# A hybrid state-space and latent-attention layer on one core: mask rows in q and k, the query latent normalised ahead of its projection, gated squares summed by TensorE, a new order table, and idle matmuls at the end

## The chip, the core and the metric

The kernel runs on one core of one Trainium2 chip. The time is device microseconds (us) of one execution. An execution is profiled apart from the timed runs; its span goes from the first to the last instruction of the core.

## What is computed

One layer for 576 tokens (512 of a new prompt, 64 of a running stream with 256 cached positions), width 1024, fp32:

```
proj = rmsnorm(x) @ w_in                    # z 512 | xBC 1024 | dt 8 | cq 256 | ckv 128 + rope 32
y    = ssd_scan(conv(xBC), dt)              # 8 state-space heads
y    = rmsnorm((y + d_skip*x) * silu(z))    # gate, then a norm over 512 channels
q    = rmsnorm(cq) @ w_uq                   # 8 heads, 64 + 32 rotated
s    = q . keys * scale, masked by blocks of 64 positions; softmax; o = pr @ values
x    = x + [y, o] @ w_out
x    = x + (silu(h @ w_gate) * (h @ w_up)) @ w_down      # h = rmsnorm(x), 2816 wide
out  = rmsnorm(x)
```

Outputs are the layer's result, the new latent keys, the rotated keys and the state-space and convolution states.

## The kernel before

Tokens lie along the free axis and channels on the 128 partitions, so a product with a weight tile is a matmul of 128 columns of weights with two halves of 288 tokens. Each such product is made of three matmuls, since weights and activations are each split in a rounded high part and a rest (`hilo`, L142 to L146, and `weights`, L112 and L113). The gate and up projections save one product in eight by sums of their operands (`xop`, L779 to L786, and `gu`, L795 to L806).

The stages follow each other in this order: the first products of the input projection and their norms, the remaining input projection with the convolution, the z part with the state-space chunks, the projection of q and k of the first head pairs and the values, the softmax of four head pairs beside the products with w_out (`ps_o`), the sums for gate and up, the gate and up products and the down products in parts, and a final norm in two column parts of 320 and 256 tokens.

Five engines work on this, each with its own queue, strictly in order. What stands where in each queue is fixed by the table `ISSUE`: a list of program numbers for each engine, which `issue_in_order` turns into a fixed sequence. DMAs are issued by SP, POOL and ACT.

What the change touches:

- `gate` (L552 to L559): the state-space output is multiplied with silu(z) on VectorE (L556), squared on ACT (L558), and the four channel tiles of the squares are added by a VectorE reduction into `ssy` (L559; the trace shows its buffer as R). `norm_y` (L728 to L732) then sums over the 128 partitions with a matmul by ones for each half (`ps_ny`, L731).
- `pair_proj` (L581 to L605): for each pair of heads, `qs` and `ks` hold 64 content and 32 rope rows. `evac_q` (L594) takes the projected q out of PSUM and multiplies with `Rq`, the norm factor of the query latent and the scale; `evac_k` (L598) copies k on ACT. The rope rows of q come by four POOL DMAs (L588), those of k by one SP DMA.
- `scores` (L634 to L651): one matmul for each query block and head (L641, contraction over 96 rows), then a VectorE memset (L642) that writes -1e30 into the 64x64 corner that the mask closes.
- `soft` (L620 to L632): maximum on VectorE (L627), exponential with sum on ACT (L628), reciprocal and scaling on VectorE (L629, L631). Score tiles live in the three PSUM banks with the tag "sc"; a fourth score matmul waits until the exponential has read the first.
- `cat_tile` (L735) scales the state-space output with its norm factor `Ry` and splits it in the two parts of `cat_y` (L142, L144), which `ps_o` reads.
- `q_rope` (L397 to L413): two products `ps_qr` for the rotated part, each taken out of PSUM with a multiplication by `Rq` (L403), then six VectorE operations.
- the end (L1040 to L1095): the squares of the second column part are summed over partitions into one packed bank (`ps_n`, L1040), a short chain on ACT and VectorE makes the factor `Rp`, two banks `ps_r` spread it again by matmuls with rows of the identity (L1091), R is copied (L1092), and VectorE and POOL scale the output, which DMAs carry out.

Of the kernel before, what the change touches and what calls it, by code (L numbers as in the profile page):

```python
# [19 lines left out]
P = 128  # L20
# [34 lines left out]
def hybrid_layer_kernel(ctx: ExitStack, tc: tile.TileContext, a, o):  # L55
# [207 lines left out]
    def in_tile(t, m=P):  # L263
# [6 lines left out]
    k1, k2, kr1, kr2, kt, rr0, rr1, qt0, qt1 = (  # L270
        rotp.tile([P, T], F32, name=z) for z in ("k1", "k2", "kr1", "kr2", "kt", "rr0", "rr1", "qt0", "qt1")
# [23 lines left out]
    dve.tensor_scalar(Rq, Rq, SCALE, None, ALU.mult)  # L295
    dve.scalar_tensor_tensor(ckf[:, :T], ckr, col(C_KN), Rk, ALU.mult, ALU.mult)
# [255 lines left out]
    def gate(c):  # L552
# [6 lines left out]
        dve.tensor_reduce(ssy[:, tk], q.rearrange("p t l -> p l t"), AX, ALU.add)  # L559
# [486 lines left out]
    with tc.manual_schedule(engines={pe.engine, dve.engine, pool.engine, act.engine}):  # L1046
# [39 lines left out]

        pr1 = [lbank("sc", f"ps_r3_{z}", 1) for z in range(2)]
# [32 lines left out]
0-7 20-21 14-15 8-13 22-25 38-39 26-29 16-19 32-37 30-31 44-47 40-43 56-61 74 48-49 62-66 75-77 50-55 68 78 69 67  # L1120
80-83 79 70-73 86-89 92-97 84-85 98 110-115 128 134-135 90-91 104-109 122-127 142-146 129-133 148-153 147 99-103
116-121 136-141 154-171 174-182 270-274 172-173 183-269 275-370 373-415 371 416-420 372 421-612 637-640 613-617
641-642 657-660 618-636 665-702 643-644 703-712 661-663 713-722 763 723-742 664 764-766 645-652 743-760 653-656
761-762 771-794 767-770 795-828 837-844 851 829-831 833-834 872-873 832 835-836 854-856 845 874-875 846-848 852-853
849-850 857-859 880-883 888-891 884-887 860-862 913-914 863-871 876-879 892-900 915-916 923-925 917-922 926 901-903
927-928 904-912 946 929-933 947-948 934-943 949-950 944 951 945 952-957 985 969 958-965 997-1001 966-968 1002-1003
973-975 986-996 1004-1008 1011-1016 970-971 976-978 1025-1027 972 979-983 1017-1019 1041-1046 984 1028-1036 1020
1009-1010 1021-1024 1037-1038 1057-1061 1063-1067 1062 1068-1074 1039-1040 1047 1050-1052 1075-1079 1048-1049
1053-1055 1103-1105 1056 1087-1092 1080-1082 1093 1083-1086 1097-1101 1106-1114 1094-1096 1141-1143 1102 1139
1144-1150 1152-1157 1151 1140 1158 1115-1126 1159-1160 1127-1138 1161-1162 1166-1169 1163-1165 1172-1173 1211-1231  # L1130
1174 1232-1234 1175-1177 1170-1171 1187-1188 1178-1180 1235-1237 1247-1252 1238-1244 1181 1209 1184 1253-1255
1182-1183 1185-1186 1210 1245-1246 1256-1258 1189 1197-1202 1190-1196 1203-1205 1259-1260 1271-1282 1261 1206 1262
1207-1208 1283-1288 1263-1270 1289-1310 1324-1337 1311-1323 1338-1510 1518-1525 1557 1511 1526-1529 1554 1560
1512-1517 1558-1559 1530-1553 1561-1562 1578-1581 1555 1563-1565 1569-1571 1590-1592 1611-1613 1582-1583 1602-1604
1556 1575-1577 1596-1598 1617-1619 1584 1623-1624 1585-1586 1572-1574 1593-1595 1566-1568 1587-1589 1608-1610
# [150 lines left out]
```

## Time and profile before

| | |
|---|---|
| runs timed | 666.59, 667.73, 669.0 us; median 667.73 |
| the profiled execution | 667.77 us, its span 666.0 us, mean granted TensorE clock 0.986 |
| busy share of the span | TensorE 97%, VectorE 79%, ACT 49%, POOL 5% |
| chain that ended last, by engine | TensorE 84%, VectorE 10%, ACT 2%, issue 2%, DMA 1%, POOL 1% |

The granted clock is given as a share of 2.4 GHz: 1.00 is 2.4 GHz and 0.50 is 1.2 GHz. In rows of the trace, "[0.64 <-ACT pr L628]" is idle time just before a group of instructions and the instruction that ended it. A group's name is output<-inputs with its shapes, and "x4" is the count of instructions. An fp32 matmul shows as two instructions.

### The profile page before, as it was taken

The page shows a single profiled execution, that of the slowest core. Times are in us where ns is not written, and L with a number is a line of the kernel's source. Part 1 is how long each engine was busy: PE and PEld are TensorE (multiplying, and loading weights), DVE is VectorE, ACT ScalarE, POOL GpSimd, SP SyncE. Part 2 cuts the span into 40 slices and gives each one's busy share as a digit, 9 for nine tenths or more (in the row PEclk, how much of TensorE's full clock was granted, in tenths as well). Part 3 has the DMA queues.
Part 4 walks back from the last instruction along what each step waited for, and adds up shares of the span by engine and source line. Part 5 has one row for each costly group of instructions (what it writes and reads, how often), then busy time and mean ns, then how long its engine had stood idle before and what let it go on. Part 6 is the DMA issues. An engine that isn't in the chain of part 4 may idle for free.

```text
span 666.0 us, 11869 instructions
## 1 busy us (share of the span) xinstructions
PE 646.1 (97%) x4691; PEld 610.5 (92%) x4691; DVE 526.0 (79%) x994; ACT 329.0 (49%) x600; POOL 31.9 (5%) x72
## 2 busy tenths in 40 slices
PE   9999999997999998999999999999999999999994
PEld 9799999864778898999999999999999999999994
DVE  6998997999878599999978585775868586966563
ACT  8644437755564367647423454324533354335463
POOL 0010230101010000000000000000000000000004
PEclk9999999996999999999999999999999999999997
DMA  9323284331042333132411233321232224222004
GB/s 324 109 69 99 63 215 131 111 99 34 32 125 64 78 98 110 64 127 73 150 64 64 72 115 100 127 64 64 80 112 95 95 64 127 65 95 95 1 0 143
DMA packets 26184, 63.61 MB, mean 96 GB/s; under 512 B 3330, under 2 KB 10000, under 8 KB 25872
## 3 DMA queue, kind: packets, MB, share of 16 engines
q1 hardware_dynamic: 24144, 60.54, 29.4%
q0 software_dynamic: 752, 1.09, 0.7%
q10 hardware_dynamic: 1232, 1.23, 0.6%
q8 instruction: 37, 0.61, 0.4%
q14 instruction: 19, 0.16, 0.1%
HBM read 58.03 MB, written 3.30 MB: 92 GB/s over the span
## 4 chain that ended last, share of the span: by engine, by line
PE 84%; DVE 10%; ACT 2%; issue 2%; DMA 1%; POOL 1%; POOLq 0%; DVEq 0%; ACTq 0%
PE ps_x L838 19%; PE ps_d L939 17%; PE ps_z L838 9%; PE ps_in L128 8%; PE ps_y L838 5%; PE ps_z L432 4%; PE ps_o L432 3%; PE ps_first L128 3%; PE sc L641 2%; PE ps_l L939 2%; PE pv L689 2%; PE ptp L664 1%; DVE xop L786 1%; DVE fz L154 1%; DMA gu<-in_w_gu 1%
## 5 line engine op out<-in xcount | busy, mean ns | idle before, releaser
L939 PE MATMUL ps_d<-pr,wh_d 128*128 128x288 f32 x576 | 115.6, 294 | 0.0
L838 PE MATMUL ps_x<-xop,wh_gu_S 128*128 128x288 f32 x504 | 101.9, 295 | 0.3 <-ACT g L900 0.3
L939 PEld LDWEIGHTS ps_d<-pr,wh_d 128*128 128x128 f32 x576 | 92.5, 188 | 0.0
L939 PE MATMUL ps_d<-pr,wl_d 128*128 128x288 f32 x288 | 84.7, 295 | 0.0
L838 PEld LDWEIGHTS ps_x<-xop,wh_gu_S 128*128 128x128 f32 x504 | 80.6, 188 | 0.5 <-ACT g L900 0.5
L113 DVE TENSOR_TENSOR wl_gu_S<-gu,wh_gu_S 128x1024 fp32r<-128x1024 f32 x44 | 53.8, 1222 | 33.7 <-PE ps_y L838 13.8
L838 PE MATMUL ps_x<-xop,wl_gu_S 128*128 128x288 f32 x252 | 73.4, 295 | 0.0
L112 ACT CAST wh_gu_S<-gu 128x1024 fp32r<-128x1024 f32 x44 | 46.1, 1051 | 44.7 <-PE ps_d L939 25.4
L939 PEld LDWEIGHTS ps_d<-pr,wl_d 128*128 128x128 f32 x288 | 54.1, 188 | 0.0
L838 PEld LDWEIGHTS ps_x<-xop,wl_gu_S 128*128 128x128 f32 x252 | 47.0, 188 | 0.0
L112 ACT CAST wh_d<-wr_d 128x640 fp32r<-128x640 f32 (+1 forms) x32 | 21.6, 675 | 48.4 <-PE ps_x L838 23.6
L128 PE MATMUL ps_in<-xs,wh_in 128*128 128x288 f32 x256 | 45.4, 298 | 0.0
L838 PE MATMUL ps_z<-xop,gu_a 128*128 128x288 f32 x252 | 38.7, 296 | 0.0
L128 PEld LDWEIGHTS ps_in<-xs,wh_in 128*128 128x128 f32 x256 | 37.8, 189 | 0.3
L838 PE MATMUL ps_z<-xop,wh_gu_S 128*128 128x288 f32 x168 | 36.3, 296 | 0.0
L838 PE MATMUL ps_x<-xop,wh_gu_A 128*128 128x288 f32 x168 | 35.5, 297 | 0.0
L838 PEld LDWEIGHTS ps_z<-xop,gu_a 128*128 128x128 f32 x252 | 35.3, 188 | 0.1
L838 PE MATMUL ps_y<-xop,wh_gu_A 128*128 128x288 f32 x168 | 35.1, 296 | 0.0
L952 DVE TENSOR_TENSOR x<-ps_d,x 128x288 f32<-128x288 f32 x64 | 28.6, 452 | 6.6 <-PE ps_d L939 6.2
L800 ACT CAST gu_a<-gu 128x512 fp32r<-128x512 f32 x22 | 13.7, 621 | 37.6 <-PE ps_x L838 18.0
L112 ACT CAST wh_gu_A<-gu 128x1024 fp32r<-128x1024 f32 x22 | 23.1, 1048 | 18.3 <-PE ps_d L939 11.5
L113 DVE TENSOR_TENSOR wl_gu_A<-gu,wh_gu_A 128x1024 fp32r<-128x1024 f32 x22 | 26.9, 1221 | 5.2 <-PE ps_x L838 3.9
(328 smaller groups left out, 1625.7 us busy)
## 6 DMA issues: line engine op xcount, KB each, us to landing
gu<-in_w_gu SPq DMA_DIRECT2D x44, 512.0 KB, 3.9
wr_d<-in_w_down SPq DMA_DIRECT2D x16, 320.0 KB, 3.0
wr_in<-in_w_in SPq DMA_DIRECT2D x8, 512.0 KB, 4.6
wr_out<-in_w_out SPq DMA_DIRECT2D x8, 512.0 KB, 3.3
wr_d<-in_w_down SPq DMA_DIRECT2D x16, 256.0 KB, 2.7
cumb<-cumD SPq DMA_DIRECT2D x5, 512.0 KB, 5.2
x<-in_xT SPq DMA_DIRECT2D x2, 1152.0 KB, 7.0
wr_z<-in_w_in SPq DMA_DIRECT2D x4, 512.0 KB, 4.5
```

What stands on the lines that cost most here:

```text
L112: act.copy(hi, raw)
L113: dve.tensor_tensor(lo, raw, hi.bitcast(F32), ALU.subtract)
L128: pe.matmul(ps[:m, hf, :n], w, x[:, hf * n : (hf + 1) * n], start=start and k == 0 and i == 0, stop=stop and k == last and i == 2,)
L154: dve.tensor_tensor(ssq, ssq, q, ALU.add)
L432: pe.matmul(ps[:, :n], w, x[:, cols], start=k == 0 and i == 0, stop=k == len(terms) - 1 and i == 2,)
L641: pe.matmul(s[:, :nk], qs[:, j, q0 : q0 + P], ks[:, j, :nk], start=True, stop=True)
L664: pe.transpose(pp[:, k : k + P], prs[p, i][:, j, b * P : b * P + P], ident)
L689: pe.matmul(pv[64 * j : 64 * j + 64, b * P :], V[b][:, h * HD : (h + 1) * HD], pts[p, b, j], start=b == 0, stop=True, skip_group_check=b > 0,)
L800: act.copy(l(a22), r(r2))
L838: pe.matmul(ps, p, q, start=not onto and first and kp == kps[0] and j == 0, stop=onto or (last and kp == kps[-1] and j == 2), skip_group_c ...
L939: pe.matmul(ps, w, x[:, cols], start=first and k == 0 and i == 0, stop=last and k == len(terms) - 1 and i == 2,)
L952: dve.tensor_tensor(x2[t][:, cols], ps, x2[t][:, cols], ALU.add)
```

## The change

The core of the diff, line numbers of the new kernel being higher by 11 to 15 from the attention on:

```diff
+    qk_bufs = [
+        (qkp.tile([100, 2, T], F32, name=f"qs{i}"), qkp.tile([100, 2, NKEY], F32, name=f"ks{i}")) for i in range(2)
+    ]
+    for z, n, v, k0 in ((0, T, -1e30, 0), (1, NKEY, 1.0, 64)):
+        m = qk_bufs[0][z][96:100]
+        pool.memset(m, v)
+        for sign in (1, -1):
+            pool.affine_select(
+                out=m, in_=m, pattern=[[0, 2], [sign, n]], compare_op=ALU.is_ge, fill=0.0,
+                base=-k0 if sign > 0 else k0 + 63, channel_multiplier=-128 * sign,
+            )
+        pool.dma_start(qk_bufs[1][z][96:100], m)
...
     dve.tensor_scalar(Rq, Rq, SCALE, None, ALU.mult)
+    dve.tensor_tensor(cq, cq, Rq.unsqueeze(1).to_broadcast([P, 2, T]), ALU.mult)
...
-            dve.tensor_tensor(halves(rr[i]), ps[:, :, :TH], Rqh, ALU.mult)
+            rr.append(ps[:, :, :TH])
...
+        for i, (f, g, u, op) in enumerate(((c0, c1, qt0, ALU.subtract), (c1, c0, qt1, ALU.add))):
+            dve.tensor_tensor(halves(s[:, i]), rr[0], f, ALU.mult)
+            dve.tensor_tensor(halves(u), rr[1], g, ALU.mult)
+            dve.tensor_tensor(s[:, i], s[:, i], u, op)
...
         act.activation(q, yv, AF.Square)
-        dve.tensor_reduce(ssy[:, tk], q.rearrange("p t l -> p l t"), AX, ALU.add)
+        ps = bank("pp", f"ps_g{c}")[:, :L]
+        for t in range(4):
+            pe.matmul(ps, ones, q[:, t], start=t == 0, stop=t == 3)
+        act.copy(ssy[:, tk], ps)
...
-        qs = qkp.tile([96, 2, T], F32, tag="qs", name=f"qs{p}")
-        ks = qkp.tile([96, 2, NKEY], F32, tag="ks", name=f"ks{p}")
+        qs, ks = qk_bufs[p % 2]
...
-        sp.dma_start(ks[64:96], krall.unsqueeze(1).to_broadcast([ROPE, 2, NKEY]))
+        if p < 2:
+            sp.dma_start(ks[64:96], krall.unsqueeze(1).to_broadcast([ROPE, 2, NKEY]))
...
-                r = slice(64 * j, 64 * j + 64)
-                dve.tensor_tensor(qs[0:64, j, cols], ps[r], Rq[r, cols], ALU.mult)
+                (dve.tensor_copy if j else act.copy)(qs[0:64, j, cols], ps[64 * j : 64 * j + 64])
...
-                dve.memset(s[0:64, nk - 64 : nk], -1e30)
...
     def norm_y():
-        ps = [bank("hm", f"ps_ny{hf}") for hf in range(2)]
         for hf in range(2):
-            pe.matmul(ps[hf][:, :TH], ones, ssy[:, hf * TH : (hf + 1) * TH], start=True, stop=True)
-            norm_half(Ry[:, hf * TH : (hf + 1) * TH], ps[hf][:, :TH], 512)
+            cols = slice(hf * TH, (hf + 1) * TH)
+            norm_half(Ry[:, cols], ssy[:, cols], 512)
...
+        warm = bank("hm", "ps_warm_last")
+        for _ in range(7):
+            pe.matmul(warm[:, :P], ones, ones, start=True, stop=True)
...
 ISSUE = {
     "PE": """
-0-7 20-21 14-15 8-13 22-25 38-39 26-29 16-19 32-37 30-31 44-47 40-43 56-61 74 48-49 62-66 75-77 50-55 68 78 69 67
+0-7 14-15 8-9 20-23 16-17 10-13 26-27 24-25 38-42 18-19 32-37 43 56 28-31 44-45 57-61 74-79 92 46-49 62-67 80-84 50-55
...
```

Each mask row r of `qs` holds -1e30 on the first 64 queries of block r and 0 elsewhere, each of `ks` holds 1 on the last 64 keys of block r, so that the score matmul over 100 rows adds -1e30 where the memset wrote it. The two pairs of buffers are used in turn by the four head pairs, so the mask rows and the rope rows of the keys stay.

The new table moves work on every engine. At the start of the softmax TensorE's queue stood like this before, with the last products of q of the second head pair (`ps_q`) between scores of the first (`sc`), and the first norm sum (`ps_ny`); the score `sc_3_0` stands four rows further ahead:

```order
L641 MATMUL sc_3_1_1916<-ks_1745,qs_1744 128x512
L641 MATMUL sc_1_0_1941<-ks_1745,qs_1744 128x256
L432 MATMUL ps_q_0_1867<-cqn_470,wl_pair_1804 128x288
L432 MATMUL ps_q_0_1867<-cqn_473,wh_pair_1803 128x288 x2
L432 MATMUL ps_q_0_1867<-cqn_473,wl_pair_1804 128x288
L432 MATMUL ps_q_1_1882<-cqn_470,wh_pair_1803 128x288 x2
L432 MATMUL ps_q_1_1882<-cqn_470,wl_pair_1804 128x288
L432 MATMUL ps_q_1_1882<-cqn_473,wh_pair_1803 128x288 x2
L432 MATMUL ps_q_1_1882<-cqn_473,wl_pair_1804 128x288
L641 MATMUL sc_1_1_1944<-ks_1745,qs_1744 128x256
L641 MATMUL sc_2_0_1957<-ks_1745,qs_1744 128x384
L731 MATMUL ps_ny_1891<-R_99,ones 128x288
```

So three scores of the first pair stood ahead of the end of its neighbour's q. In the new kernel the queue is, from the end of the same product on, with the gated sums of the last two chunks as `ps_g`:

```order
L443 MATMUL ps_q_1_1912<-cqn_484,wl_pair_1826 128x288
L654 MATMUL sc_3_0_1939<-ks_383,qs_382 128x512
L654 MATMUL sc_3_1_1941<-ks_383,qs_382 128x512
L572 MATMUL ps_g_1876<-ysq_1874,ones 128x128
L654 MATMUL sc_1_0_1965<-ks_383,qs_382 128x256
L654 MATMUL sc_1_1_1967<-ks_383,qs_382 128x256
L572 MATMUL ps_g_1885<-ysq_1883,ones 128x128 x4
L654 MATMUL sc_2_0_1979<-ks_383,qs_382 128x384
L654 MATMUL sc_2_1_1981<-ks_383,qs_382 128x384
L654 MATMUL sc_0_0_1993<-ks_383,qs_382 128x128
L572 MATMUL ps_g_1876<-ysq_1874,ones 128x128 x3
```

All scores of the first pair now stand behind the last product of q, the gated sums stand between them, and the two norm sums are gone.

VectorE's queue at the same place before (evacuations of q, memsets, maxima `mx`, gated sums into R_99):

```order
L594 TENSOR_TENSOR qs_1807<-ps_q_0_1867,Rq 64x288
L642 MEMSET sc_3_1_1916 64x64
L594 TENSOR_TENSOR qs_1807<-ps_q_0_1867,Rq 64x288
L642 MEMSET sc_1_0_1941 64x64
L627 TENSOR_REDUCE mx<-sc_3_1_1916 128x1
L559 TENSOR_REDUCE R_99<-ysq_1858 128x128
L594 TENSOR_TENSOR qs_1807<-ps_q_1_1882,Rq 64x288
L642 MEMSET sc_1_1_1944 64x64
L627 TENSOR_REDUCE mx<-sc_1_0_1941 128x1
```

and in the new kernel:

```order
L607 COPY qs_384<-ps_q_0_1897 64x288
L567 TENSOR_TENSOR xsd<-xsd,sz 128x4x128
L640 TENSOR_REDUCE mx<-sc_3_0_1939 128x1
L567 TENSOR_TENSOR xsd<-xsd,sz 128x4x128
L640 TENSOR_REDUCE mx<-sc_3_1_1941 128x1
L640 TENSOR_REDUCE mx<-sc_1_0_1965 128x1
L607 COPY qs_384<-ps_q_1_1912 64x288
L640 TENSOR_REDUCE mx<-sc_1_1_1967 128x1
```

The reductions and memsets are gone, of each two evacuations one is left, and the last gated multiplication (L567) stands behind the first maximum.

At the end of the program TensorE's queue is now this, where before the two `ps_r` followed the packed sums directly:

```order
L1051 MATMUL ps_n_1_7355<-fz,ones 64x128 x2
L1051 MATMUL ps_n_1_7355<-sq,ones 64x128 x4
L1100 MATMUL ps_warm_last<-ones 128x128 x7
L1106 MATMUL ps_r_0_7545<-Rp,ident 128x128 x2
L1106 MATMUL ps_r_1_7546<-Rp,ident 128x128 x2
```

The seven idle matmuls multiply ones with ones, and nothing reads their result.

## Rows read from the trace of the kernel before

**Rows 1.** The page, busy time by engine
```profile
PE 646.1 (97%) x4691; PEld 610.5 (92%) x4691; DVE 526.0 (79%) x994; ACT 329.0 (49%) x600; POOL 31.9 (5%) x72
```
**Rows 2.** Stretches: length, busy PE, PEld, DVE, ACT, POOL, clock, DMA share, GB/s
```profile
140.00:148.00 8.00, 7.76 (x37) 5.46 (x35) 7.80 (x16) 4.14 (x9) 0.00 (x0) 1.00 0.52 154
148.00:154.00 6.00, 3.44 (x11) 1.59 (x11) 5.77 (x16) 4.56 (x13) 0.00 (x0) 1.00 0.17 69
154.00:166.00 12.00, 9.77 (x27) 4.94 (x26) 11.57 (x35) 5.68 (x17) 2.25 (x4) 0.57 0.18 48
166.00:226.00 60.00, 60.00 (x422) 48.47 (x422) 47.41 (x141) 32.81 (x90) 1.92 (x4) 1.00 0.20 62
...
234.00:271.00 37.00, 34.22 (x248) 32.77 (x247) 36.86 (x67) 26.27 (x41) 0.00 (x0) 1.00 0.26 88
```
**Rows 3.** Waits of TensorE: total us, times, longest
```profile
PE sc L641 <- ACT pr L628: 3.0, 5, 1.1
...
PE ps_p L838 <- DVE xop L786: 1.8, 3, 1.1
```
**Rows 4.** Timeline of TensorE, 143 to 180 us: start, us, group
```profile
143.24 1.12 PE L641 MATMUL sc<-ks,qs 96*128 96x512 f32 x2
...
147.80 0.29 PE L432 MATMUL ps_q<-cqn,wl_pair 128*128 128x288 f32 x1
...
165.72 0.51 PE L432 MATMUL ps_o<-cat_y,wh_out 128*128 128x288 f32 x2
...
171.52 0.49 PE L664 MATMUL ptp<-ident,pr 128*128 128x128 f32 x3
...
172.96 0.71 PE L664 MATMUL ptp<-ident,pr 128*128 128x128 f32 x5
```
**Rows 5.** Timeline of VectorE, 133 to 169 us
```profile
145.92 0.69 DVE L627 TENSOR_REDUCE mx<-sc 128x1 f32<-128x512 f32 x1
...
166.61 0.76 DVE L144 TENSOR_TENSOR cat_y<-xsd,cat_y 128x576 fp32r<-128x576 f32 x1 [1.00 <-ACT cat_y L142]
...
167.47 0.73 DVE L144 TENSOR_TENSOR cat_y<-xsd,cat_y 128x576 fp32r<-128x576 f32 x1
```
**Rows 6.** Single lines: count, ns min/median/max, first and last start
```profile
L559 DVE TENSOR_REDUCE R<-ysq x5: 593/1031/1074, 133.5 to 152.5; 128x128 f32<-128x512 f32 x4, 128x64 f32<-128x256 f32 x1
...
L594 DVE TENSOR_TENSOR qs<-ps_q,Rq x16: 431/454/461, 136.8 to 193.6; 64x288 f32<-64x288 f32 x16
...
L642 DVE MEMSET sc<- x32: 112/112/112, 144.5 to 214.4; 64x64 f32 x32
...
L731 PE MATMUL ps_ny<-R,ones x4: 403/406/481, 151.2 to 154.0; 128*128 128x288 f32 x4
```
**Rows 7.** Groups by form: busy us, mean ns, idle before
```profile
L403 DVE TENSOR_TENSOR rr<-ps_qr,Rq 128x576 f32<-128x576 f32 x2 | 1.5, 754 | 0.6 <-PE ps_qr L128 0.6
...
L489 POOL TENSOR_SCALAR_AFFINE_SELECT cumb<-cumb 128x1024 f32<-128x1024 f32 x4 | 4.4, 1093 | 22.2 <-ACT el L464 22.2
...
L322 POOL MEMSET dt<- 128x40 f32 x1 | 0.1, 132 | 23.4 <-DVE wl_in L113 23.4
```
**Rows 8.** Timeline of VectorE, 218 to 283 us
```profile
233.95 0.69 DVE L795 TENSOR_TENSOR gu<-gu 128x512 f32<-128x512 f32 x1 [1.56 <-DMA gu<-in_w_gu]
...
271.16 2.09 DVE L786 TENSOR_TENSOR xop<-xv,xop 128x576 fp32r<-128x576 f32 x3
```
**Rows 9.** Timeline of all engines, 651 us to the end
```profile
657.40 2.08 PE L1091 MATMUL ps_r<-Rp,ident 128*128 128x128 f32 x8 [1.90 <-DVE Rp L178]
...
659.51 0.37 ACT L1092 COPY R<-ps_r 128x256 f32<-128x256 f32 x1 [2.89 <-PE ps_r L1091]
```
**Rows 10.** Stretch of the end, columns as in rows 2
```profile
658.00:659.50 1.50, 1.48 (x7) 1.18 (x6) 0.84 (x3) 0.00 (x0) 0.00 (x0) 0.50 0.55 194
```
**Rows 11.** Timeline of TensorE, the first 5 us
```profile
1.00 3.78 PE L203 MATMUL ps_warm<-ones 128*128 128x128 f32 x16 [1.00 <-POOL nepsb L97]
```
**Rows 12.** Timeline of ACT, 143 to 170 us
```profile
148.58 0.62 ACT L558 ACTIVATE ysq<-xsd 128x512 f32<-128x512 f32 x1
```

More of the change, by code (lines that the diff above doesn't have):

```diff
@@ L246, in hybrid_layer_kernel @@
     ssq2, ssk = tmp("ssq2"), tmp("ssk")
+    Rq = tmp("Rq")
     for k in range(2):
@@ L267, in in_tile @@
         return ps[:m, :, :TH]
-    k1, k2, kr1, kr2, kt, rr0, rr1, qt0, qt1 = (
-        rotp.tile([P, T], F32, name=z) for z in ("k1", "k2", "kr1", "kr2", "kt", "rr0", "rr1", "qt0", "qt1")
+    k1, k2, kr1, kr2, kt, qt0, qt1 = (
+        rotp.tile([P, T], F32, name=z) for z in ("k1", "k2", "kr1", "kr2", "kt", "qt0", "qt1")
     )
@@ L398, in q_rope @@
         w = weights(a["w_uqr"], 512, "uqr")
-        rr = (rr0, rr1)
+        rr = []
         for i in range(2):
@@ L1125 @@
[L1125 to L1134, printed above, removed]
@@ new lines @@
+146-147 154-171 174-175 270-274 176-221 172-173 222-269 275-370 373-420 371 421-468 372 469-636 665-688 637-638
+641-644 639-640 657-658 689-735 737-742 736 743-760 659-660 645-656 661-664 771-818 763 767-770 764-766 761-762
+819-826 859-861 833-835 837 862-864 838 836 827-832 865-866 868-870 867 880-883 841 845-852 871-873 853-856 839-840
+842-844 874-876 884 877-879 885-886 904-909 857 887 858 888 892-899 910-912 900-903 889-891 913-915 925-926 916-924
+927-935 939-940 949-951 936-938 952-965 941 966-967 945-948 968-970 942-944 971-979 987 980-983 1003 988 1015-1016 984
@@ new lines @@
+991-993 985-986 989 1004-1009 1017-1021 1010-1011 1022-1024 1012-1014 1025-1026 994-999 1029-1034 1043-1045 1000-1002
+990 1046-1054 1035-1042 1059-1064 1027-1028 1075-1079 1055 1081-1092 1080 1065 1056 1066 1057 1067 1058 1093-1104 1068
+1121-1129 1069-1073 1130-1132 1105-1107 1133-1144 1074 1145-1156 1108 1229-1240 1111-1113 1119 1109-1110 1241-1246
+1253-1254 1114 1247-1248 1120 1157 1255-1260 1249-1252 1158 1115-1118 1159-1160 1261-1263 1161 1264 1176 1162-1175
+1177 1180 1265 1178 1184-1186 1181-1183 1187 1190-1192 1266-1274 1179 1188 1275-1276 1193-1198 1189 1199-1207
@@ new lines @@
+1215-1220 1208-1214 1221-1222 1227-1228 1277-1288 1223 1289-1296 1224-1226 1301-1303 1297-1300 1304-1322 1342-1343
+1348-1355 1344-1347 1323-1341 1356-1479 1572 1575 1480-1496 1573 1497-1523 1578 1524-1535 1574 1576 1536-1538
+1579-1580 1539-1547 1584 1581-1582 1587 1585 1599 1583 1548-1552 1577 1560 1602-1604 1553-1559 1561-1563 1588-1589
+1564-1571 1593-1595 1614-1616 1635-1637 1608-1610 1629 1586 1605-1607 1626-1628 1647 1590-1592 1611 1630-1631 1650
+1612-1613 1632 1648-1649 1600-1601 1620-1622 1641-1643 1596-1598 1617-1619 1638-1640 1651 1623-1625 1644-1645 1656
@@ new lines @@
+222 225 216-217 211 220 218 212-213 226 219 221 301 233 227-228 223 234 229-232 237 235 245 236 246 256 238 257 247
+316 248-249 261 258 262 260 239 266 259 240 267 263 241 265 264 242 271 243 268 244 269-270 274 250 252 275 272 251
+273 254 253 279 255 280-281 296 283 276 297 282 302 284 293 288 294 289 285 287 277-278 304 327 290-291 298 315 286
+305 328 306 292 310 326 311 329 312 307 303 337 314 317 313 318 338 378 321 299-300 309 308 339 332 379 322 330 333
+323 319 334 380 331 340-341 320 325 336 348 335 342 344-345 343 346-347 324 383 349 353 350 358 352 354 364 351 365
@@ new lines @@
+355 381 360 356 366 393 371 382 359 367 357 373 361 374 370 368-369 384 362 375-376 363 377 372 386-387 385 388-389
+392 391 390 398 406 394 399 395 400 402 401 403 413 396 404 421 397 405 409 407 411 410 412 419 408 415 417 414 416
+418 436 420 424 422 425 423 426 429 427-428 432-434 431 478 485 437 435 439 430 440 438 441 480 442-443 481 444 454
+479 447-448 450 449 452 451 453 445 455 458 456 446 457 459 482-483 460 467 462 484 461 468 463 489 469 471 470 464
+493 491 486 465 564 472 490 492 494 473 496 504 488 474 495 497 505-506 508 487 569 501 576 507 466 589 475 503 509
@@ new lines @@
+198-199 203 212 222 215 214 213 218 228 206 229-230 254 231-232 219-220 226 221 255 225 224 227 235 234 233 236-240
+242 245-246 241 247 261 250 243-244 248-249 252-253 251 256-258 260 259 267 263-265 268 270 266 276 269 274 262
+271-272 285 273 275 277-278 283 280-281 279 282 312 284 286 313 287 292 288-289 293 295 291 294 290 296 299 297-298
+300-301 314 302-303 315 319 304-305 320 306-308 316 309 318 317 321-323 328-329 326 330 327 310 331-332 324 337 311
+338 335 339 336 341 340 333 346-347 344-345 348 325 334 349 357-358 342 350 354 351 343 359 353 352
@@ L1185 @@
+65 67 66 76 71 70 78 69 73 64 86-87 75 74 88 80 84-85 89-91 98 101 99-100 102-103
 """,
```

82 lines of the change are left out of this document (25 added, 57 removed).

## The prediction

> **What bounds the kernel now.** I read the busy shares, then the stretches, then the waits of TensorE, and last the timelines where it waits. TensorE is busy 97% of the span [rows 1], so a gain can only come from the few places where it waits or runs at the lower clock. The stretches show them [rows 2]. Up to 148 us and from 166 to 226 us it is full, and the clock is at 1.00. From 148 to 154 us it is busy 3.44 of 6 us, and from 154 to 166 us the granted clock is 0.57 on average, that is mostly 1.2 in place of 2.4 GHz. VectorE is busy 5.77 of 6 and 11.57 of 12 us there: this is the start of the softmax, where VectorE has maxima, scaling, gated sums, evacuations and the norm of the state-space output at once. TensorE's largest wait is there too: 3.0 us in which score matmuls wait until the exponential frees a bank [rows 3], and the exponential waits for VectorE's maximum. From 234 to 271 us VectorE is busy 36.86 of 37 us, and the gate and up products wait 1.8 us for their summed operands [rows 2, 3]. At the end the two `ps_r` run 2.08 us in eight instructions, at a clock of 0.50, after an idle time of 1.90 us [rows 9, 10]. Behind 271 us and ahead of 148 us nothing is to be had from order alone.
>
> **The softmax start, before.** The last product of q ends at 148.1 us, the first maximum starts at 145.92, the fourth split of `cat_y` ends at 168.20, and the products with w_out run densely from 165.72 [rows 4, 5]. So VectorE takes 22.28 us from the first maximum to the fourth split, with 1.00 us idle.
>
> **What the change adds on TensorE.** An fp32 matmul of 128 columns is two instructions; five such take 0.71 and three 0.49 us, so each adds 0.11 us [rows 4]. A gated sum of a full chunk is four matmuls, 8 x 0.11 = 0.88 us, the half chunk half of it: 4.5 chunks are 3.96 us. The `ps_ny` go: two matmuls, four instructions of 0.25 us each in steps, 1.0 us (a single one is listed with 406 ns, of which the overlap is taken off) [rows 6]. Net 2.9 us. 2.5 chunks (2.2 us) lie ahead of the end of q, where TensorE is full, but three score tiles (512, 512 and 256 columns, 2 x 10 pieces of 128 columns x 0.11 = 2.2 us) move behind it. So q ends again at about 148.0, and the added 2.9 us fall in the stretch in which TensorE has room: 6 - 3.44 us up to 154 alone.
>
> **What it takes from VectorE.** Four gated reductions of 1.03 and one of 0.59 us (4.7 us), half of the 16 evacuations of 0.45 (3.6 us), and 32 memsets of 0.11 us, which mostly overlap and which I count at 0.06 (1.9 us) [rows 6]. ACT gets eight copies; it is busy 49% [rows 1], and only 4.56 of 6 us in the tightest stretch [rows 2]. Of these savings the ones in full stretches count. After the first maximum: two gated sums 1.9, three of four evacuations 1.2, ten memsets 0.6, the idle 1.0 (the splits now have ACT's part further ahead), together 4.7. Against it one more 128x512 maximum in front of the splits, 0.6, and a gated multiplication less, 0.6. So 22.3 - 4.7 = 17.6 us; summing the new queue's instructions by the same durations gives 17.0. I take 17.3. The first maximum cannot start until `sc_3_0` is done: 148.0 + 0.9 + 0.1 = 149.0 us. The fourth split then ends at 166.3, not 168.2: **-1.9 us**. Behind it, TensorE's remaining work up to the next common point is 0.66 us less, since pair 1's scores have been moved ahead: I take 0.5. **Sum for this stage: -2.4 us.** The ends: nothing, if the chain is as long as before; and -6.8 if TensorE alone decides: its work from the end of q to `ps_o` is 34 pieces of 128 score columns x 0.22, the sample scores 0.5, two gated sums 1.76 and eight transposes 1.76, 11.5 us, so `ps_o` at 159.6 in place of 165.72, and the 0.66. The value lies nearer to VectorE's sum, since VectorE is the one that is full in these rows.
>
> **166 to 226 us.** TensorE is full, VectorE 47.41 of 60 us [rows 2]. 22 memsets and eight evacuations leave VectorE; hidden, so 0. The shift passes through.
>
> **234 to 271 us.** The stage begins when the first gate and up weights land, at 233.95, and the last summed operands are done at 273.25 [rows 8]: 39.3 us of VectorE. Priced with the steps at which the same kinds follow each other there, the new queue has 0.8 us less ahead of the last operand: a weight split of the following group now stands behind it, and running sums of squares stand elsewhere. **-0.8 us**; bounds 0 and -1.8, the whole wait [rows 3].
>
> **The end.** The seven idle matmuls follow the packed sums at 655.50 and take 14 x 0.11 = 1.5 us, up to 657.0, ahead of the 657.40 at which `Rp` is there [rows 9]. TensorE is then idle 0.4 in place of 1.90 us. If the clock stays at 1.00, `ps_r` takes 8 x 0.13 = 1.04 and not 2.08 us; R's copy, the last scaling and the DMAs behind it move with it: **-1.0 us**. The Trainium skill has a rule that speaks against this (TensorE: Matmul & The Clock Gate, section "The HAM clock gate"): the clock falls after a whole window without work, so one short gap would not lower it, and the idle matmuls would be worth nothing. The row shows 0.50 behind a gap of 1.90 us, so the measurement decides; by the page the term would be 0.
>
> **Costs I set to nothing.** The mask rows: POOL gets two memsets, four selections and two DMAs at the start. A selection over 1024 elements takes 1.09 us, so 4 x 1.1 to 1.8, with the memsets under 9 us, inside the 23.4 us in which POOL waits for the time-step rows [rows 7]; key DMAs queued behind them are needed far later. If that cover were gone, the first scores would wait for `ks`. Four more contraction rows: 0. The query norm: one multiplication over 1152 columns, twice 0.75 less the overlap, 1.4 us, against the two of 0.754 that go [rows 7]; the normalised latent must now wait for its norm factor, and its last part stands some fifteen VectorE instructions ahead of the one that reads the first product made of it. `ps_qr` stays longer in PSUM; VectorE is next to read it. Two SP DMAs go. New orders ahead of 148 us: 0, TensorE has no room there to gain.
>
> **Sum:** -2.4 - 0.8 - 1.0 = -4.2 us on the profiled execution's 667.77 us, which is as good as the median (667.73): **663.5 us**. About 2 us, 0.3%, is what a measurement of this kernel can tell from no change.
>
> **Rivals.**
>
> *The clock falls again (0.20).* In 148 to 154 us TensorE was busy 57% of the time and the clock fell after it [rows 2]. The new order has 11.5 us of work up to `ps_o`, about 70% of the time, but still in short groups that wait for banks. If half of it runs at 1.2 GHz, that adds 5.7 us: 148.0 + 11.5 + 5.7 = 165.2, only 0.5 to 1 us better than now; with 0.8 and 1.0 that is 665.3. The Trainium skill names such a case on the same page (section "A second HAM failure mode: psum-queue depth-cycling"): groups that cycle through PSUM banks leave TensorE idle for short times, and the clock goes up and down. Rows 2 agree with it for the kernel before.
>
> *The chain of the softmax is not shorter (0.13), and the kernel slower.* TensorE's queue now holds `ps_g_1885` between score tiles. It waits for ACT's square of a gated product that stands on VectorE behind the first maximum: 149.0 + 0.6 + 0.6, then the square of 0.62 [rows 12], and about as much for an exponential ahead of it: 151.5. The scores `sc_2_0` and later stand behind it. If the round from bank to maximum to exponential sets the pace and not VectorE's sum, the chain keeps its 22.3 us but starts at 149.0, not 145.92 [rows 5]: +3.1, with -1.0 at the end and nothing at 234 us, 669.9. It decides if VectorE shows idle times of over 4 us in sum between the first maximum and the fourth split.
>
> *TensorE decides (0.12).* -6.8, -1.8 and -1.0: 658.2. For it: VectorE loses 4.7 us exactly where it is full. Against: the scaled probabilities still come late in VectorE's queue.
>
> *The idle matmuls run slowly (0.07).* At the start of the kernel 16 such instructions took 3.78 us, 0.236 each [rows 11]. 14 of them would end at 658.8, 1.4 us after `Rp`: 667.77 - 3.2 + 1.4 = 666.0.
>
> **How the numbers follow.** My forecast has 0.48. Its own range is 661.5 to 665.7: the chain's 17.0 to 17.6, the middle term 0 to -1.8, the end 0 to -1.0. Faster by over 0.3% (under 665.7) takes in nearly all of it, the third rival and half of the first: 0.69. Slower by over 0.3% (over 669.8) is half of the second rival and a little for waits that a new order of five queues may open anywhere: 0.13. The rest, 0.18, is no change. The range 659 to 669 leaves out half of the second and half of the third rival and the unnamed.
>
> **What would show it.** In the changed profile: first maximum at about 149, fourth split at about 166, `ps_o` dense from about 163, granted clock 1.00 through 154 to 166 us; `ps_r` in about 1.0 us at a clock of 1.00; the last summed operand some 3 us earlier than 273.25. A clock near 0.5 at the softmax, or VectorE idle there, would put the first term wrong; `ps_r` still at 2 us the last; a TensorE wait over 1 us ahead of 148 us the assumption that the new order costs nothing.

## The result and the profile after

The changed kernel takes **656.54 us** (median of 4 runs, 655.98 to 659.61) where the kernel before took 667.65 beside it: ratio **0.984 [0.981, 0.988]**, 11.1 us faster. The forecast was 663.5 us in a range of 659 to 669: the sign was right, the time lies below the range, and the gain is 2.6 times the one forecast. The profiled execution after took 656.87 us, its span 655.2, which is 10.8 us less than the span before; the steps below are made from the two spans.

The page, busy time by engine, of the kernel after:

```profile
PE 641.5 (98%) x4741; PEld 612.5 (93%) x4741; DVE 516.0 (79%) x948; ACT 332.7 (51%) x613; POOL 43.8 (7%) x80
```

Against [rows 1] TensorE has 4.6 us less and VectorE 10 us less, but the shares hardly move. Stretches of the kernel after, columns as in [rows 2]:

```profile
148.00:154.00 6.00, 6.00 (x28) 3.58 (x27) 5.88 (x14) 5.27 (x15) 0.00 (x0) 1.00 0.94 310
154.00:166.00 12.00, 10.00 (x53) 6.58 (x51) 11.99 (x32) 9.16 (x27) 2.01 (x4) 1.00 0.29 106
166.00:226.00 60.00, 60.00 (x435) 47.94 (x434) 43.71 (x114) 31.80 (x91) 1.91 (x4) 1.00 0.16 52
226.00:265.00 39.00, 38.29 (x286) 37.76 (x286) 38.98 (x72) 28.20 (x43) 0.00 (x0) 1.00 0.25 89
```

At the softmax start TensorE is now busy 6.00 of 6 us (3.44 before) and the clock stays at 1.00 where it was 0.57; from 148 to 166 us it issues 81 instructions where it issued 38. VectorE is as full as it was, 11.99 of 12 us. The waits of TensorE, kernel after:

```profile
PE ps_in L128 <- DVE sp_a L350: 1.3, 1, 1.3
...
PE sc L654 <- ACT pr L641: 1.0, 3, 0.5
PE ps_p L849 <- ACT xop L796: 0.7, 1, 0.7
```

The wait for score banks is 1.0 us, not 3.0, that of `ps_p` 0.7, not 1.8 [rows 3]. A new one of 1.3 us stands at about 60 us (`ps_in` for the time-step chain), the sign that the prediction named for a new order that is not free. It costs some tenths: the last q product of the second pair ends at 148.6 us, 148.1 before. With the same queues up to there, the runs below show it with 0.4 to 1.6 us.

VectorE's timeline after, at the places of [rows 5] and [rows 8]: the first maximum, two maxima of the second pair, the last two splits of `cat_y`, the first sum of gate and up weights with the addition ahead of it, and the last summed operands.

```profile
149.58 0.69 DVE L640 TENSOR_REDUCE mx<-sc 128x1 f32<-128x512 f32 x1
...
159.44 0.68 DVE L640 TENSOR_REDUCE mx<-sc 128x1 f32<-128x512 f32 x1
...
161.49 0.68 DVE L640 TENSOR_REDUCE mx<-sc 128x1 f32<-128x512 f32 x1
...
165.24 1.59 DVE L144 TENSOR_TENSOR cat_y<-xsd,cat_y 128x576 fp32r<-128x576 f32 x2
...
225.89 0.46 DVE L732 TENSOR_TENSOR x<-ps_o,x 128x288 f32<-128x288 f32 x1 [0.41 <-PE ps_o L443]
226.27 0.68 DVE L806 TENSOR_TENSOR gu<-gu 128x512 f32<-128x512 f32 x1
...
262.54 2.08 DVE L797 TENSOR_TENSOR xop<-xv,xop 128x576 fp32r<-128x576 f32 x3
```

The first maximum moved back by 3.7 us, yet the fourth split ends at 166.83, 1.4 us sooner than the 168.20 before. The end, TensorE's timeline:

```profile
646.27 1.83 PE L1100 MATMUL ps_warm_last<-ones 128*128 128x128 f32 x14
648.24 1.16 PE L1106 MATMUL ps_r<-Rp,ident 128*128 128x128 f32 x8
```

`ps_r` takes 1.16 us, where it took 2.08 behind a gap [rows 9], and the copy of R starts 1.20 us behind its start, not 2.11.

Where the 10.8 us come from, by events that both traces have (us from the start of the span):

| event | before | after | shift | forecast at this point |
|---|---|---|---|---|
| fourth split of `cat_y` ends | 168.21 | 166.83 | -1.4 | -1.9 |
| first gate/up load is issued (behind all scores) | 227.78 | 222.29 | -5.5 | -2.4 |
| first gate/up sum starts | 233.95 | 226.27 | -7.7 | -2.4 |
| last summed operand ends | 273.25 | 264.62 | -8.6 | -3.2 |
| `ps_r` starts | 657.40 | 648.24 | -9.2 | -3.2 |
| copy of R starts | 659.51 | 649.44 | -10.1 | -4.2 |
| end of the span | 665.99 | 655.16 | -10.8 | -4.2 |

So the forecast was right up to the fourth split, in the operand stage (-0.95 for -0.8) and at `ps_r` (-0.9 for -1.0). Two steps gave far more than forecast: 4.1 us between the fourth split and the gate/up load (0.5 forecast), and 2.2 us from that load's issue to the first sum (0 forecast). Part of the latter is chance: a further profile of the old program up to there (old_idle below, which differs only behind 650 us) has the fourth split at 167.81, the load at 227.38 and the first sum at 232.12, 4.7 us behind the load's issue and not 6.2. So the steps between events are good to some tenths, the landing to 1.5 us. Where a step starts scatters more: the five profiles below that have the changed kernel's queues up to the first maximum show it between 149.28 and 150.25 us.

### The profile page after: what moved, and what is told of

Its sections match the earlier page's. It is cut to its first block, busy times and chain, and to the rows that moved or that the text cites. A ratio compares the mean times of both kernels' runs of the same rounds, so it can differ in the third digit from the quotient of the medians.

```text
span 655.2 us, 11919 instructions
## 1 busy us (share of the span) xinstructions
PE 641.5 (98%) x4741; PEld 612.5 (93%) x4741; DVE 516.0 (79%) x948; ACT 332.7 (51%) x613; POOL 43.8 (7%) x80
## 4 chain that ended last, share of the span: by engine, by line
PE 68%; DVE 6%; ACT 1%; issue 1%; POOL 1%; POOLq 0%; DVEq 0%
PE ps_x L849 20%; PE ps_d L950 17%; PE ps_z L849 10%; PE ps_y L849 5%; PE ps_o L443 5%; PE ps_l L950 2%; PE sc L654 2%; PE pv L701 2%; PE ptp L676 1%; PE ps_p L849 1%; DVE xop L797 1%; DVE fz L154 1%; DVE x L732 1%; PE ps_q L443 1%; DVE pr L644 0%
## 5 line engine op out<-in xcount | busy, mean ns | idle before, releaser
L1086 POOL TENSOR_TENSOR fz<-fz,sq 128x256 f32<-128x256 f32 x6 | 4.4, 738 | 456.9 <-ACT sq L1082 456.7
```

## Experiments

Times of different sittings aren't compared directly; each ratio is to the kernel before, run beside it. The changed kernel's interval is wide (0.9807 to 0.9877): of the kernels made from it only gates_on_dve, masks_by_memset and new_order_old_work lie clear of it in time, and smaller effects are read from the traces alone. Sizes within the program are taken from the profiled spans (`after` 655.2). Where a part of the change is undone, the new table is kept and the instructions that come back are put where their inputs are ready.

### The end: idle matmuls alone, away and added

```diff
-        warm = bank("hm", "ps_warm_last")
-        for _ in range(7):
-            pe.matmul(warm[:, :P], ones, ones, start=True, stop=True)
```

Away from the changed kernel (no_idle):

> The changed kernel without its seven idle matmuls at the end. My theory: the granted clock falls to 0.50 before the last two products, which take 2.1 us and not 1.16; R is copied about 1 us later than in the changed kernel, counted from the start of Rp, and the time is 657.5 in place of 656.5. Rival (the rule by which one short gap leaves the clock alone): the products take 1.0 to 1.2 us, no difference. Everything ahead of 646 us is unchanged.

657.27 us, ratio 0.9863 [0.9847, 0.9878]. TensorE's timeline and the stretch behind the gap:

```profile
648.01 1.99 PE L1102 MATMUL ps_r<-Rp,ident 128*128 128x128 f32 x8 [1.90 <-DVE Rp L178]
```
```profile
648.00:650.00 2.00, 1.99 (x8) 1.70 (x8) 0.81 (x3) 0.00 (x0) 0.00 (x0) 0.53 0.73 255
```

R's copy starts 2.03 us behind `ps_r`, 1.20 with the idle matmuls: they are worth 0.8 us at that point. That this reaches the end isn't shown: the spans are 655.3 us without them and 655.2 with them. Added to the kernel before (old_idle):

> The kernel before with the seven idle matmuls alone. My theory: the last two products take 1.1 in place of 2.08 us at a clock of 1.00, and the time falls from 667.7 to 666.7. Rival: the idle matmuls run at half clock, end behind Rp and cost up to 1.4 us: 669.

666.06 us, 0.9992 [0.9983, 1.0002]. Its `ps_r` takes 1.16 us and R follows at 1.19, so the mechanism works there too. But from R's copy to the end its profiled run needs 6.65 us, where before needed 6.48, after 5.72 and no_idle 5.30, with the same scaling and output DMAs: this last stretch scatters by as much as the idle matmuls bring. The -0.8 us between R and the end in the table above is therefore no effect of the change that I could show.

### The landing of the gate and up weights

One line of the table moves: VectorE's split of the last w_out load but one goes back behind a copy that stands later (late_split).

```diff
 L678 COPY pt_2_2532<-ptp_2_1_2538 128x384
-L113 TENSOR_TENSOR wl_out_0_2789<-wr_out_0_2786,wh_out_0_2788 128x1024
...
 L686 COPY pts_2719<-ptp_s 128x256
+L113 TENSOR_TENSOR wl_out_0_2789<-wr_out_0_2786,wh_out_0_2788 128x1024
```

> The changed kernel with one VectorE instruction moved back to where it stood before: the split of the first w_out weight of the second half (wl_out of the tile read at 225.41 in the trace of before) stands again behind the last copy of transposed probabilities. The load that takes over its buffer, 512 KB, is then issued right ahead of the first gate and up weights. My theory: these land 2 us later (6 in place of 4 us behind their issue), the summed operands and all behind them come 1.5 to 2.2 us later, the time is 658 to 658.7. Rival: the load is hidden, VectorE has enough else to do while it waits; no difference (656.5).

658.61 us, 0.9883 [0.9868, 0.9898]. SP's queue in the kernel before, in this one, and in the changed kernel (time from the issue's start until SP goes on, and what it issues):

```profile
213.24 13.79 SPq L119 DMA_DIRECT2D wr_out<-in_w_out  x2
227.78 0.33 SPq L792 DMA_DIRECT2D gu<-in_w_gu  x1
```
```profile
204.75 18.23 SPq L119 DMA_DIRECT2D wr_out<-in_w_out  x2
223.07 0.39 SPq L803 DMA_DIRECT2D gu<-in_w_gu  x1
```
```profile
211.19 0.33 SPq L119 DMA_DIRECT2D wr_out<-in_w_out  x1
222.29 0.33 SPq L803 DMA_DIRECT2D gu<-in_w_gu  x1
```

Before, SP stands until 227.0 us in front of a 512 KB w_out load whose buffer VectorE frees only with the split at 225.41 us; that load then goes out right ahead of the first gate/up weights, and their first sum starts 6.2 us after their issue (4.7 in old_idle, 5.5 in old_clock_held, with the same queue). After, the split runs at 209.95, the load leaves at 211.19, and the first sum starts 4.0 us after the issue, as in all kernels here that have the new table with the early split (3.97 to 4.07). With the split back at 221.38 the row of 18.23 us is there again, VectorE waits 1.07 us for the weights, and their first sum starts 5.0 us behind the issue, at 228.11. The first of the two loads itself lands 3.7 us after its issue in the changed kernel, 4.9 with the split back, 6.1 before. **This is shown**, with a size of 1.1 us at the first sum. All behind it is 1.8 us late, but 0.7 us of that stood there ahead of the moved split already (first maximum at 150.25 us for 149.58), so that the time came as expected is in part luck. The reverse in the kernel before (old_early_split: that split and its cast on ACT earlier, nothing else):

> The kernel before with that one split, and the ACT rounding that it waits for, moved some 6 us ahead. My theory: the first gate and up weights land 4 us behind their issue at 227.8 and not 6.2, VectorE's sums start at 232 in place of 233.95, and the time falls by 1.5 to 2.2 us to about 666. Rival: no difference, or slower, since the split delays the last values on VectorE.

666.0 us, 0.9994 [0.9985, 1.0003], inconclusive in time, and not the 1.5 to 2.2 us expected. The load lands 3.7 us after its issue at 228.61, as in the changed kernel, but the first sum starts 4.5 us after it, not 4.0:

```profile
232.76 0.46 DVE L720 TENSOR_TENSOR x<-ps_o,x 128x288 f32<-128x288 f32 x1 [0.99 <-PE ps_o L432]
233.13 0.68 DVE L795 TENSOR_TENSOR gu<-gu 128x512 f32<-128x512 f32 x1
```

Once the load is there in time, the sum starts when VectorE comes to it, behind an addition that waits for a product with w_out, here as in the changed kernel (225.89 and 226.27 us). So about 0.5 of the 2.2 us belongs to the new order of this end of the stage, and not to the load. The load is also issued 0.8 us later than before; 0.3 of it stood at the fourth split already, ahead of the moved split, and the rest I did not settle.

### Which of the three savings of VectorE counts

Gated sums back to VectorE (gates_on_dve):

```diff
-        ps = bank("pp", f"ps_g{c}")[:, :L]
-        for t in range(4):
-            pe.matmul(ps, ones, q[:, t], start=t == 0, stop=t == 3)
-        act.copy(ssy[:, tk], ps)
+        dve.tensor_reduce(ssy[:, tk], q.rearrange("p t l -> p l t"), AX, ALU.add)
...
+            ps = bank("hm", f"ps_ny{hf}")[:, :TH]
+            pe.matmul(ps, ones, ssy[:, cols], start=True, stop=True)
```

> The changed kernel with the gated sums as VectorE reductions again and the two norm sums as matmuls, all else in the new order. My theory: VectorE is what limits the start of the softmax, so the 4.7 us that come back (2 us of them behind the first maximum) delay the splits of cat_y by 2 to 3 us, and the clock may fall again between 154 and 166 us: 658.5 to 661. Rival (the order gives the gain, the gated sums on TensorE only cost their 2.9 us): 654 to 656.5.

The memset ahead of each maximum again, the mask rows kept (masks_by_memset), and all q copies on VectorE (evac_on_dve):

```diff
+                dve.memset(s[0:64, nk - 64 : nk], -1e30)
```

> The changed kernel with the 32 memsets of the masked corners back ahead of each maximum; the mask rows stay, so the result is the same. My theory: ten of them lie in the full stretch of VectorE and cost 0.06 to 0.11 us each there, and each makes its maximum wait one step more: 657 to 658 in place of 656.5. Rival: hidden beside the neighbours, 656.5.

```diff
-                (dve.tensor_copy if j else act.copy)(qs[0:64, j, cols], ps[64 * j : 64 * j + 64])
+                dve.tensor_copy(qs[0:64, j, cols], ps[64 * j : 64 * j + 64])
```

> The changed kernel with all sixteen copies of q out of PSUM on VectorE, none on ACT. My theory: eight more copies of 0.45 us on VectorE, three or four of them in the full stretch: 657 to 658. Rival: ACT's share was on the path just as well, or VectorE has room: 656.5 or less.

All three undone (new_order_old_work; the norm of the query latent and the idle matmuls stay new):

> The new order with the old work: gated sums and all copies of q on VectorE, memsets back, norm sums as matmuls. The query norm ahead of the projection and the idle matmuls stay. My theory (the work taken from VectorE gives the gain of the softmax start, the order that of the weights that land sooner): most of the first part is lost, 661 to 664, and the clock falls between 154 and 166 us. Rival (the new order alone makes the difference): 656 to 658.

Measured, with events of the profiled run in us:

| kernel | time | ratio to before | first maximum | fourth split | from there to the gate/up load | span |
|---|---|---|---|---|---|---|
| before | 667.65 | 1 | 145.92 | 168.21 | 59.57 | 666.0 |
| after | 656.54 | 0.9842 [0.9807, 0.9877] | 149.58 | 166.83 | 55.46 | 655.2 |
| gates_on_dve | 664.0 | 0.9955 [0.994, 0.997] | 151.38 | 170.97 | 56.05 | 659.9 |
| masks_by_memset | 661.37 | 0.9914 [0.9899, 0.993] | 150.24 | 169.56 | 57.40 | 659.8 |
| evac_on_dve | 658.86 | 0.9878 [0.9862, 0.9895] | 151.30 | 168.91 | 56.02 | 657.8 |
| new_order_old_work | 668.67 | 1.002 [1.0009, 1.0032] | 153.59 | 175.48 | 58.36 | 666.7 |

All four came out above what my theories had. Each saving counts in the traces; for the copies of q alone the intervals of the times overlap. Of gates_on_dve the profile shows the shortest of five executions (661.65 us at a mean granted clock of 0.993, the others 663.0 to 664.5 at 0.989), so its row understates the gated sums. The new table with the old work is no faster than before, rather 0.2% slower. So the table alone gives no gain; the work taken from VectorE does, in a table that was laid out for it. The old table with the new work was not run, and what the work gives without the table stays open. All three at once delay the first maximum by 4.0 us and the fourth split by another 4.6. The stretch without the savings:

```profile
154.00:166.00 12.00, 8.25 (x19) 3.96 (x20) 11.71 (x35) 7.62 (x24) 0.33 (x1) 0.65 0.55 192
```

VectorE full, TensorE at a clock of 0.65 with 19 instructions, where the changed kernel has 53. The memsets cost 4.6 us of span, where I had counted 0.06 each for ten of them. VectorE's timeline of masks_by_memset shows why:

```profile
150.09 0.11 DVE L655 MEMSET sc<- 64x64 f32 x1
150.24 0.69 DVE L640 TENSOR_REDUCE mx<-sc 128x1 f32<-128x512 f32 x1
150.84 0.68 DVE L567 TENSOR_TENSOR xsd<-xsd,sz 128x512 f32<-128x512 f32 x1
151.53 0.11 DVE L655 MEMSET sc<- 64x64 f32 x1
151.68 0.69 DVE L640 TENSOR_REDUCE mx<-sc 128x1 f32<-128x512 f32 x1
```

The product at 150.84 starts 0.09 us before the maximum ahead of it ends (150.24 + 0.69); the memset starts only behind the product's end (151.53 against 150.84 + 0.68), and the maximum behind it 0.04 us after the memset's. So a memset of 0.11 us lengthens the row by 0.15 and the lost overlap, 0.23 us.

### Memsets at the softmax start, and behind it

The prediction had priced these two differently, so they were put back apart (masks_at_start, masks_after_start).

```diff
+                if p == 0 or (p == 1 and i == 3):
+                    dve.memset(s[0:64, nk - 64 : nk], -1e30)
```

The other part has `if p > 1 or (p == 1 and i < 3)` in its place.

> The changed kernel, with the memset put back ahead of ten maxima only: the eight of pair 0 and the first two of pair 1, all ahead of the fourth split of cat_y. The mask rows stay, so each memset is only work for VectorE. Theory 1 (at the softmax start every microsecond of VectorE's queue is a microsecond of the kernel): in the run with all 32 memsets a memset starts 0.15 us ahead of its maximum, and the overlap of about 0.08 us with the instruction ahead of it is lost as well, so 0.23 us each and 2.3 us at the fourth split (about 169.1 us against 166.83); the time 2.3 to 3.3 us above the changed kernel's, most of the 4.8 us that all 32 cost. Theory 2 (they cost because TensorE later stands behind maxima that hold the score banks longer, 166 to 222 us): at most 1 us here.

> The other part: the memset ahead of the remaining 22 maxima, all behind the fourth split, where TensorE is full and VectorE busy 42 of 56 us. Theory 1: hidden, as the prediction counted them: 0, at most 1 us, and the fourth split as in the changed kernel, 166.8 us. Theory 2: 3 to 4 us, with waits of TensorE for maxima or for VectorE's copies between 166 and 222 us. If this run and the one with the ten add up to much less than 4.8 us, the two parts cost only together.

| kernel | time | ratio to before | first maximum | fourth split | from there to the gate/up load | span |
|---|---|---|---|---|---|---|
| masks_at_start (10) | 659.21 | 0.9873 [0.9856, 0.989] | 149.30 | 168.64 | 55.49 | 657.0 |
| masks_after_start (22) | 658.95 | 0.9868 [0.9852, 0.9885] | 149.48 | 166.74 | 57.41 | 657.0 |

Both theories hold for half. The ten, VectorE's timeline at the first maximum and the last two splits:

```profile
149.30 0.69 DVE L640 TENSOR_REDUCE mx<-sc 128x1 f32<-128x512 f32 x1
...
167.05 1.59 DVE L144 TENSOR_TENSOR cat_y<-xsd,cat_y 128x576 fp32r<-128x576 f32 x2
```

From the first maximum to the fourth split these are 19.34 us, where the changed kernel has 17.25: the nine memsets that stand there cost 2.1 us, 0.23 each, as theory 1 had it. (The fourth split is only 1.8 us later, since the first maximum came 0.3 us sooner in this run.) The 22 cost nearly as much, 1.9 us, all behind the fourth split, 0.09 each, where theory 1 had them hidden, in a stretch in which VectorE is not full. In these steps the two parts add up to the 32 (masks_by_memset: 19.32 and 57.40 us). The stretch with the 22:

```profile
178.00:220.00 42.00, 41.22 (x283) 32.39 (x282) 34.02 (x103) 23.21 (x66) 1.92 (x4) 1.00 0.17 55
```

TensorE stands 0.78 us there, 0.6 of it in front of `pvs`, for a copy of VectorE; the changed kernel shows 42.00 busy in the same stretch. The other 1.1 us show as no idle time: laid against the changed kernel, the same instructions run ever later from 178 to 205 us, in steps of about 0.25 us. What holds TensorE in those steps stays open.

### The clock without the work

Is the low clock of [rows 2] itself the loss? The kernel before got 26 idle matmuls between its scores, on TensorE alone (old_clock_held).

```diff
+        warm = bank("pp", "ps_warm_mid")
+        for _ in range(26):
+            pe.matmul(warm[:, :P], ones, ones, start=True, stop=True)
```

> The kernel before, with 26 idle matmuls (128 columns, 0.22 us each at full clock) put between its score tiles from 149 to 163 us, where TensorE waits for banks; nothing reads them, and no other engine's queue changes. Theory 1 (VectorE's queue sets the start of the softmax, the low clock is only its companion): the fourth split stays within 0.7 us of 168.2, and the time within 0 to -1.5 us of before. Theory 2 (the low clock itself is the loss, 154 to 166 us at 0.57 on average, so that scores and transposes take twice as long): granted clock near 1.00, the fourth split 2 us or more sooner, and the time 3 to 6 us below before. Lost if the idle matmuls delay scores: above before.

```profile
148.00:154.00 6.00, 5.20 (x28) 3.74 (x27) 5.77 (x15) 4.71 (x14) 0.00 (x0) 1.00 0.19 77
154.00:166.00 12.00, 11.08 (x73) 8.55 (x74) 11.97 (x36) 6.41 (x18) 1.95 (x4) 1.00 0.19 48
```

The clock is at 1.00 in both stretches, and the time 666.23 us, 0.9985 [0.9972, 0.9997]: the fourth split comes at 167.32, 0.5 to 0.9 us sooner than in old_idle and before, the gate/up load 0.7 to 1.1 us, and no more. So the low clock is worth about 1 us; VectorE's queue sets the pace, and the clock follows from it. masks_after_start says the same from the other side: up to the fourth split it runs the changed kernel's queues, its clock from 154 to 166 us was 0.86, and its fourth split ended at 166.74, no later than with 1.00.

### One more step off VectorE

If VectorE's queue is the pace, 0.95 us less should bring about 1 us (norm_half_on_pool). GpSimd idles there, so it got the first half of `Ry`.

```diff
-            norm_half(Ry[:, cols], ssy[:, cols], 512)
+            norm_half(Ry[:, cols], ssy[:, cols], 512, ve=dve if hf else pool)
...
+                pool.tensor_scalar(u, u, 1.5, None, ALU.add)
+                pool.tensor_tensor(R, u, y0, ALU.mult)
```

> The changed kernel, with the three VectorE steps that make the first half of Ry (scale and shift, product, the last scaling; about 0.95 us of VectorE between 155.2 and 157.0 us) done by GpSimd, in four instructions. Theory 1: GpSimd idles there, so VectorE's queue is 0.95 us shorter: fourth split at about 165.9, time 0.9 to 1.5 us below the changed kernel's 656.5. Rivals: VectorE's chain is by now set by the round of exponentials and not by its own sum (ACT shows no idle from 149.6 to 158.9 us either): 0; or GpSimd's instructions slow VectorE's down, or end after 158.2 us, where the first product with Ry would start: up to 1 us slower.

658.14 us, 0.9858 [0.9839, 0.9877]: not better. The fourth split ends at 167.40, 0.6 us later. GpSimd's timeline, then VectorE's beside it:

```profile
155.96 0.79 POOL L178 TENSOR_TENSOR nr_u<-nr_u,nr_v 128x288 f32<-128x288 f32 x1 [1.92 <-issue]
156.85 1.16 POOL L182 TENSOR_SCALAR nr_u<-nr_u 128x288 f32<-128x288 f32 x1
158.09 0.79 POOL L183 TENSOR_TENSOR Ry<-nr_u,nr_y 128x288 f32<-128x288 f32 x1
```
```profile
156.79 0.91 DVE L649 TENSOR_SCALAR pr<-pr,sm 128x384 f32<-128x384 f32 x2
157.62 0.55 DVE L173 TENSOR_SCALAR nr_v<-R 128x288 f32<-128x288 f32 x1
158.09 0.47 DVE L645 TENSOR_REDUCE mx<-sc_s 128x1 f32<-128x320 f32 x1
158.63 0.56 DVE L178 TENSOR_TENSOR nr_u<-nr_u,nr_v 128x288 f32<-128x288 f32 x1
```

The same VectorE instructions take 0.73, 0.29 and 0.44 us in the changed kernel, here 0.91, 0.55 and 0.56, each while GpSimd runs; the maximum, which reads PSUM, is unchanged. GpSimd's own scalar step takes 1.16 us there and took 0.42 for the same shape at 153.6 us, when it was VectorE's scaling of 128x512 beside it that took 0.72 (0.48 in the changed kernel). That agrees in kind with the Trainium skill (SBUF — State Buffer, section "Who interferes with whom"): VectorE instructions in a two-port mode or with two SBUF inputs contend with GpSimd, and a reduction doesn't. The Trainium skill also says there that whichever of the two issues first has the shared ports for its whole instruction and the other is blocked; here both engines got longer in turn, and these rows don't show which of them was blocked when. VectorE was also idle for 0.22 us waiting for an exponential, with ACT as full as VectorE from 149.6 to 158.9 us. So both rivals have a part in it, and this run doesn't separate them. No kernel tried beats the changed one.

## Why the prediction was right or wrong

**"So 22.3 - 4.7 = 17.6 us ... I take 17.3 ... 149.0": right, in part by luck.** First maximum 149.58 for 149.0; from there to the fourth split 17.25 us for 17.3, with VectorE never idle. The mechanism is the one forecast, VectorE's sum, but its terms were not. The new queue has two 128x512 maxima more ahead of the fourth split and not one (159.44 and 161.49 us); before, both stood behind it:

```profile
168.13 0.67 DVE L627 TENSOR_REDUCE mx<-sc 128x1 f32<-128x512 f32 x1
...
169.41 0.68 DVE L627 TENSOR_REDUCE mx<-sc 128x1 f32<-128x512 f32 x1
```

That is 0.6 us that the sum lacks. The other way, the memsets were priced too low: 0.6 us for ten, where nine of them cost 2.1 in the new table. With all the old work in the new table this row is 21.9 us, so the savings are worth 4.6 there; the forecast had 3.7 for them, and 1.0 of idle time.

**"22 memsets and eight evacuations leave VectorE; hidden, so 0": the first step that failed.** Between the fourth split and the gate/up load the 22 memsets are worth 1.95 us (57.41 against 55.46), the evacuations 0.56, the gated sums another 0.59; all three undone at once give 2.9. So VectorE's work was not covered there. I had taken "TensorE full, VectorE 47 of 60 us" [rows 2] as proof of a cover. It is an average, and TensorE's 60.00 of 60 was no proof either: in the same stretch, just as full, the changed kernel has 435 matmul instructions where 422 stood, and 4.1 us were gained.

**"TensorE's remaining work is 0.66 us less ... I take 0.5": too small.** The new table with the old work needs 1.2 us less there than before (58.36 against 59.57). With the 2.9 this is the whole 4.1 us.

**"The shift passes through": the second step that failed.** I followed the work up to the last scores and not the loads behind it. A VectorE split stood late and held a w_out load on SP's queue directly ahead of the gate/up weights; the new table moves it. The first sum gains 2.2 us on its issue in these two profiles, 0.8 to 2.2 with the other profiles of the old queue; late_split takes 1.1 of it away again, and about 0.5 is VectorE coming sooner to the sum. My bound for this stage, -1.8 us from TensorE's listed wait [rows 3], looked only at waits inside the stage and could not see its start move. Inside the stage -0.95 us were measured for -0.8.

**"-1.0 us" at the end: right in size at R's copy, not shown at the end.** -0.9 at R's copy, 0.8 by no_idle; the DMAs behind it scatter by as much, and no_idle's span is only 0.1 us longer. The rule of the Trainium skill that I set against it (TensorE: Matmul & The Clock Gate, section "The HAM clock gate") would have made it 0; before and no_idle fell to 0.50 and 0.53 behind the same gap of 1.90 us. It does not fall each time, though (last section).

**"Behind 271 us and ahead of 148 us nothing is to be had from order alone": nearly.** Ahead of 148 us nothing was gained, and some tenths were lost behind a wait of 1.3 us. The mask rows took GpSimd 9.2 us and were done at 34 us, far ahead of the scores, so they cost nothing, as forecast. From the last operand to `ps_r` the changed kernel needs 383.6 us where before needed 384.15; the four profiles with the old table lie at 384.1, those with the new one between 383.5 and 383.7. So 0.5 us that I had not seen.

**Rivals.** The clock did not fall again (it shows 0.86 from 154 to 166 us in masks_after_start, at no cost). The slower chain did not come about: VectorE shows no idle time between the first maximum and the fourth split. "TensorE decides" gave 658.2, nearest to the result, but it is not what happened, since VectorE is busy 11.99 of 12 us there. The idle matmuls ran at full clock (0.13 us each).

## What to carry to other kernels

Work taken from an engine can pay also in stretches where its busy share says that there is room: put an instruction back in one stretch at a time to see what its cover is worth. Follow each queue to the first load behind the stage; a small instruction on one engine that frees a buffer late can put a large load in front of the one that everybody waits for. A low clock beside a full engine may be only its companion: hold the clock with idle matmuls, and see how little comes back, before you count on it.

## What was not expected of the hardware

- **The clock behind a short gap is not the same each time.** In old_early_split `ps_r` followed the same gap as before without any idle matmul, and ran at full clock; the row differs from [rows 9] in its length alone:

```profile
656.98 1.16 PE L1091 MATMUL ps_r<-Rp,ident 128*128 128x128 f32 x8 [1.90 <-DVE Rp L178]
```

- **A 64x64 memset in PSUM can cost twice its duration**: listed with 0.11 us, each lengthens VectorE's full row at the softmax start by 0.23 us, for the overlap that its neighbours lose; behind it, where VectorE has room, a memset still cost 0.09 us of the kernel.
